# Retention core of a two-layer hybrid trunk: a chunk's rows are normalised on ScalarE, with scale and bias made on GpSimd

## The chip, the cores and the metric

One core of a Trainium2 chip runs the whole program. The metric is device time in microseconds (us); before the change it is 3035.81 us, the median of 3 runs (3035.24 to 3036.67). TensorE is called PE in the profile, its weight loads PEld, VectorE DVE, ScalarE ACT, GpSimd POOL, and SyncE SP; SP and ACT also issue DMAs.

## The reference, cut to what matters

The trunk has two layers. Layer 0 mixes with a gated delta net, layer 1 with retention, and each is followed by a residual layer norm and a convolutional FFN. Only the retention of layer 1 is touched (4 heads, key width 256, value width 512, 8 chunks of 128 rows):

```
def retention(h, w_in, w_out):
    ...
    scores = jnp.einsum('bhncd,bhnmd->bhncm', q, k) * dmask[None, :, None]
    intra = jnp.einsum('bhncm,bhnmv->bhncv', scores, v)
    def step(state, inp):
        q_n, k_n, v_n = inp
        o = jnp.einsum('bhck,bhkv->bhcv', q_n, state) * xi[None, :, :, None]
        state = (state * gamma_c[None, :, None, None]
                 + jnp.einsum('bhck,bhcv->bhkv', k_n * zeta[None, :, :, None], v_n))
        return state, o
    ...
    o = _unchunk_heads(intra + jnp.moveaxis(inter, 0, 2))
    o = _standardize(o, 1e-6).reshape(b_, s, H * dv)
    o = o * jax.nn.silu(gate.astype(F32))
    return o.astype(h.dtype) @ w_out
```

`_standardize(o, 1e-6)` subtracts each row's mean over its 512 values and multiplies by one over the root of variance plus 1e-6. The change is in how this is done on the chip.

## The kernel before

Activations and weights are split into a high and a low part, and a product is three matmuls (low by high, high by low, high by high). In the retention stage (about 1800 to 2190 us of the span) two kinds of work share the engines:

- `ret_fill` is the filler on TensorE: the value projection `ret_v` for each head and half (weights are loaded into `wr`, split into `wh` by ScalarE and `wl` by VectorE, and the products split again into `vv`), and after the last head the first part of the output projection (`ab`, `bb`).
- `core(h)` goes through the 8 chunks of head h in order. This text numbers the chunks 0 to 31, so that chunk 7 is the last of the first head. For chunk n it makes the state update in two tiles `p2` (matmuls `sc<-vv,kz`, three for each tile), calls `ret_front` for chunk n+1 (scores `sT`, their split `sThl`, the scaled keys `kz`, and on GpSimd the scaled queries `qx`), and then makes the chunk's output `po`.
- `ret_back(h, n, po)` takes `po` (128 rows of 512, in PSUM) through the normalisation into `on`, transposes `on` on TensorE (`mm<-cst,on`), multiplies by the gate rows `gt` into `ot` on VectorE, and stores `ot`. From chunk 4 of each head on, GpSimd also makes four sums and differences of `ot` and of an earlier block `op` that is loaded again (the loop with `pool.tensor_tensor(d, x, y, op)`, written `ot<-ot`, `op<-ot,op`, `op<-op` and `ot<-ot,op` in the profile); the output projection reads these from DRAM.

`po` and `p2` share two PSUM buffers (tag `sc`). In the order of use, the second `p2` tile of a chunk takes the buffer of the `po` just before it, so its first matmul must wait until the last reader of that `po`, which is the instruction that writes `on`.

TensorE's order in this stage is written down by the kernel: `run` picks the next piece of work by a model clock, and `pm` and `ptr` chain every matmul and transpose to the one before (`pq`). The delays after which a piece may go on are the numbers `RL`; the transposes of `on` are placed `RL["b"]` = 3.21 us of model time behind `po`. None of these numbers changes. All engines take their instructions in a fixed order; that of VectorE, ScalarE, GpSimd and SP is decided when the program is built, by a scheduler that models the engines' times. So an instruction that waits on GpSimd also holds those behind it.

GpSimd has other work in the stage: `bg_gain` multiplies and adds gain rows (L381 and L382, 128x512 each) for a later residual, `qx` (L1689), and the sums above (L1775; L1777 in the changed file).

Of the kernel before, what the change touches and what calls it, by code (L numbers as in the profile page):

```python
# [11 lines left out]
AF = mybir.ActivationFunctionType  # L12
ALU = mybir.AluOpType
# [20 lines left out]
def trunk_kernel(ctx: ExitStack, tc, A):  # L34
    nc = tc.nc
    pe, act, dve, pool, sp = nc.tensor, nc.scalar, nc.vector, nc.gpsimd, nc.sync
# [9 lines left out]
    def tl(tag, shape, dt=F32, name=None):  # L46
        return sb.tile(shape, dt, tag=tag, name=name or tag, bufs=BUFS[tag])
# [7 lines left out]
    def ct(name, shape, dt=F32):  # L55
        return cp.tile(shape, dt, tag=name, name=name)
# [4 lines left out]
    def mm_tile():  # L61
        return ps.tile([P, HALF], F32, tag="mm", name="mm", bufs=2)
# [13 lines left out]
    def v4(ap):  # L76
        return ap.rearrange("p (c f) -> p c f", f=P)
# [66 lines left out]
    mhalf = ct("mhalf", [P, NCH])  # L144
# [493 lines left out]
    def ptr(out, src):  # L638
        pq(pe.transpose(out, src, ident), 0.109)
# [4 lines left out]
    def emit(name, lat=0.0):  # L644
        events[name] = clk[0] + lat
# [1046 lines left out]
    def core(h):  # L1692
# [8 lines left out]
        for n in range(NCH):  # L1701
# [25 lines left out]
            if n > 0:  # L1727
                for j in range(2):
                    pm(po, r["qx"][:, j], St[:, j], start=False, stop=(j == 1), cost=0.857)
            give("qkv", 2)  # L1730
            yield [(-0.1, ret_back(h, n, po))]
            yield RL["c"]
            St, r = Sn, rn
        emit(("core", h))

    def ret_back(h, n, po):
        st = tl("st", [P, 2, 6], name="rst")
        dve.bn_stats(st[:, 0], po)
        mv = tl("s8", [P, 4], name="mv")
        dve.bn_aggr(mv[:, 0:2], st[:, 0])  # L1740
        dve.tensor_scalar(mv[:, 2:3], mv[:, 1:2], 1e-6, None, ALU.add)
        pool.tensor_tensor(mv[:, 3:4], mv[:, 2:3], mhalf[:, 0:1], ALU.pow)
        on = tl("t2", [P, HALF], name="on")
        dve.tensor_scalar(on, po, mv[:, 0:1], mv[:, 3:4], ALU.subtract, ALU.mult)
        yield RL["b"]
        sl = slice(n * P, (n + 1) * P)
        g = tl("cv", [P, 516], name="gt")[:, 0:HALF]
        sp.dma_start(v4(g), gd[4 * h:4 * h + 4, :, sl].rearrange("j p t -> p j t"))
        pt = mm_tile()
        for j in range(4):  # L1750
            ptr(pt[:, j * P:(j + 1) * P], on[:, j * P:(j + 1) * P])
        ot = tl("cv", [P, 516], name="ot")[:, 0:HALF]
        dve.tensor_mul(ot, pt, g)
        s4 = slice(n % 4 * P, (n % 4 + 1) * P)

        def pair_view(t):
            return t.rearrange("p (j a f) -> p a j f", a=2, f=P)

        def blk(nm):
            return od[2 * h:2 * h + 2, ABLK.index(nm), :, s4].rearrange("j p t -> p j t")  # L1760

        ov = pair_view(ot)
        if n < 4:
            for a, nm in enumerate(("11", "12")):
                anchor["x", 1] = act.dma_start(blk(nm), ov[:, a])
            if n == 3:
                emit(("ob", h), RL["o"])
            return
        pv = pair_view(tl("cv", [P, 516], name="op")[:, 0:HALF])
        for a, nm in enumerate(("11", "12")):  # L1770
            sp.dma_start(pv[:, a], blk(nm))
        act.dma_start(blk("22"), ov[:, 1])
        for d, x, y, op, nm in ((ov[:, 0], ov[:, 0], ov[:, 1], ALU.add, "S1"), (pv[:, 0], ov[:, 0], pv[:, 0], ALU.subtract, "S2"),
                                (pv[:, 1], pv[:, 1], pv[:, 0], ALU.subtract, "S4"), (ov[:, 1], ov[:, 1], pv[:, 0], ALU.subtract, "S3")):
            pool.tensor_tensor(d, x, y, op)  # L1775
            sp.dma_start(blk(nm), d)
# [135 lines left out]
```

## Time and profile before

| what | value |
|---|---|
| median of 3 runs | 3035.81 us |
| span of the profiled execution (first to last instruction) | 3033.2 us |
| PE busy, share of the span | 2841.1 us, 94% |
| DVE busy | 2303.6 us, 76% |
| ACT busy | 1314.4 us, 43% |
| POOL busy | 671.3 us, 22% |
| mean granted TensorE clock | 0.977 |

The profile lists one execution. Its span is 2.6 us below the median of the timed runs; the rest of a run's time lies outside the first and the last instruction. In rows of the timeline the columns are: start, duration (both us from the span's start), engine, line, operation, output and inputs, shapes and how many instructions in a row were merged; a bracket gives the idle time of the engine just before and what ended it. In rows of the groups they are: line, engine, operation, names, shapes and count, then the total busy time and the mean in ns, then idle time before and who ended it. Rows of the waits give the total, the number of times and the longest.

### The profile page before, as it was taken

Reading aid. Unit: us, or ns where it says so; the run is one execution under the profiler, and the core shown is the slowest. Engines: PE = TensorE matmul, PEld = TensorE weight load, DVE = VectorE, ACT = ScalarE, POOL = GpSimd, SP = SyncE. Lnnn points to the kernel's source line nnn. Section 1 sums busy time; section 2 is a strip of 40 time slices with the busy share of each in tenths; the row PEclk is TensorE's granted clock in tenths of the full one; section 3 lists DMA queues with packets and bytes.
Section 4 is the critical chain, followed back from the end, with each engine's and each line's share of the span. In section 5 each row is a group of like instructions: output and inputs, shape, how many; then the busy total and the mean of one; then the engine's idle time right before and its main releaser. Section 6 shows DMA issues by size and latency. Waiting matters only on the chain.

```text
span 3033.2 us, 39037 instructions
## 1 busy us (share of the span) xinstructions
PE 2841.1 (94%) x13590; PEld 2309.7 (76%) x13590; DVE 2303.6 (76%) x3971; ACT 1314.4 (43%) x2408; POOL 671.3 (22%) x637
## 2 busy tenths in 40 slices
PE   8999899999999999998999999999998899999996
PEld 7877777877778888776777787767776678887885
DVE  5878788565888888988688645666788887777988
ACT  4745555434544444535333342222344544444442
POOL 0312211043021111820023302432200011113604
PEclk9999999999999999999999999999999999999998
DMA  7231222254354445854322544656654243335663
GB/s 275 78 122 53 77 84 78 88 176 144 107 169 149 148 150 170 316 176 154 132 100 89 174 163 138 209 178 178 214 199 150 90 144 104 105 105 202 238 192 122
DMA packets 243028, 450.23 MB, mean 148 GB/s; under 512 B 22928, under 2 KB 76432, under 8 KB 242832
## 3 DMA queue, kind: packets, MB, share of 16 engines
q1 hardware_dynamic: 211648, 400.02, 40.2%
q10 hardware_dynamic: 29760, 43.00, 3.9%
q0 software_dynamic: 1424, 4.72, 0.4%
q8 instruction: 107, 1.75, 0.2%
q14 instruction: 89, 0.73, 0.1%
HBM read 339.13 MB, written 108.53 MB: 148 GB/s over the span
## 4 chain that ended last, share of the span: by engine, by line
PE 55%; DVE 22%; DMA 11%; issue 6%; ACT 4%; POOL 2%; SPq 0%; POOLq 0%; DVEq 0%; ACTq 0%
PE acc L636 11%; PE acc L1148 7%; PE acc L110 4%; PE acc L111 4%; PE acc L112 4%; PE sc L636 4%; PE sc L1148 3%; DMA mvw<-in_ada_w 2%; PE acc L278 2%; PE acc L279 2%; PE acc L280 2%; PE mm L636 2%; DMA wr<-in_ffn_up 2%; DVE qkv L457 2%; DVE wb L90 2%
## 5 line engine op out<-in xcount | busy, mean ns | idle before, releaser
L636 PE MATMUL acc<-hT,wh 128*128 128x512 f32 x960 | 299.4, 393 | 0.0
L1546 POOL TENSOR_TENSOR o<-o 128x512 f32<-128x512 f32 x88 | 118.0, 1352 | 721.5 <-DVE o L1539 680.5
L278 PE MATMUL acc<-bb,ab 128*128 128x512 f32 x504 | 190.5, 406 | 33.5 <-DVE ab L90 20.4
L1148 PE MATMUL acc<-T,wb 128*128 128x512 f32 x840 | 206.0, 393 | 10.3 <-DVE wb L90 10.0
L279 PE MATMUL acc<-bb,ab 128*128 128x512 f32 x504 | 204.5, 406 | 8.8 <-DVE bb L90 8.5
L636 PEld LDWEIGHTS acc<-hT,wh 128*128 128x128 f32 x960 | 181.8, 189 | 34.1
L89 ACT ACTIVATE ab<-ar 128x512 fp32r<-128x512 f32 x210 | 128.6, 624 | 168.0 <-PE acc L280 83.7
L636 PE MATMUL acc<-hT,wl 128*128 128x512 f32 x480 | 201.2, 419 | 0.1
L280 PE MATMUL acc<-bb,ab 128*128 128x512 f32 x504 | 200.9, 400 | 0.0
L1148 PEld LDWEIGHTS acc<-T,wb 128*128 128x128 f32 x840 | 157.9, 189 | 48.4 <-DVE wb L90 14.7
L90 DVE TENSOR_TENSOR ab<-ar,ab 128x512 fp32r<-128x512 f32 x210 | 167.9, 809 | 34.5 <-ACT ab L89 34.1
L90 DVE TENSOR_TENSOR wl<-wr,wh 128x1024 fp32r<-128x1024 f32 x85 | 108.7, 1279 | 97.2 <-ACT wh L89 96.4
L90 DVE TENSOR_TENSOR wb<-wr,wb 128x512 fp32r<-128x512 f32 x162 | 114.5, 709 | 87.7 <-ACT wb L89 85.2
L90 DVE TENSOR_TENSOR wb<-mm,wb 128x512 fp32r<-128x512 f32 x216 | 145.0, 683 | 17.5 <-ACT wb L89 15.6
L89 ACT ACTIVATE wh<-wr 128x1024 fp32r<-128x1024 f32 x101 | 106.8, 1059 | 111.2 <-PE acc L636 43.4
L89 ACT ACTIVATE wb<-mm 128x512 fp32r<-128x512 f32 x216 | 122.8, 594 | 66.6 <-DVE mm L1194 65.5
L1205 ACT ACTIVATE pc<-acc 128x512 f32<-128x512 f32 x143 | 84.4, 592 | 147.1 <-PE acc L1148 92.5
L278 PEld LDWEIGHTS acc<-bb,ab 128*128 128x128 f32 x504 | 96.9, 194 | 62.5 <-DVE ab L90 20.3
L1525 DVE SCALAR_TENSOR_TENSOR o<-g,vc,o 128x512 f32<-128x512 f32 (+2 forms) x176 | 136.6, 795 | 5.1 <-ACT o L1520 4.5
L636 PE MATMUL acc<-wh,hT 128*128 128x512 f32 x384 | 137.2, 420 | 2.0 <-DVE vv L90 2.0
L89 ACT ACTIVATE wb<-wr 128x512 fp32r<-128x512 f32 x162 | 98.8, 626 | 87.0 <-DMA wr<-in_ffn_up 47.2
L216 DVE SCALAR_TENSOR_TENSOR ada<-mvw,e,ada 128x512 f32<-128x512 f32 x140 | 107.7, 769 | 29.0 <-DMA mvw<-in_ada_w 28.7
(636 smaller groups left out, 7855.7 us busy)
## 6 DMA issues: line engine op xcount, KB each, us to landing
wr<-in_ffn_up SPq DMA_DIRECT2D x96, 512.0 KB, 4.2
mvw<-in_ada_w SPq DMA_DIRECT2D x80, 512.0 KB, 4.3
ad<-o SPq DMA_DIRECT2D x154, 256.0 KB, 2.6
ar<-ad SPq DMA_DIRECT2D x154, 256.0 KB, 4.3
Br<-in_ffn_down SPq DMA_DIRECT2D x88, 256.0 KB, 3.7
wr<-in_ret_wv SPq DMA_DIRECT2D x32, 512.0 KB, 3.6
ar<-od SPq DMA_DIRECT2D x56, 256.0 KB, 5.3
xs<-xt ACTq DMA_DIRECT2D x24, 512.0 KB, 3.9
```

Of the source, the lines that this page charges most:

```text
L89: act.activation(dst_h, src, AF.Copy)
L90: eng.tensor_tensor(dst_l, src, dst_h, ALU.subtract)
L110: mm(acc, wl[:, k], hl[0], start=first, stop=False)
L111: mm(acc, wh[:, k], hl[1], start=False, stop=False)
L112: mm(acc, wh[:, k], hl[0], start=False, stop=last)
L278: mm(acc, a[1][:, sl], w[0], start=first, stop=False)
L279: mm(acc, a[0][:, sl], w[1], start=False, stop=False)
L280: mm(acc, a[0][:, sl], w[0], start=False, stop=last)
L636: pq(pe.matmul(out, lhsT, rhs, start=start, stop=stop), cost)
L1148: return pe.matmul(*a, skip_group_check=True, **kw)
L1525: dve.scalar_tensor_tensor(tv, gv[:, c0 - j:c1 - j], w[:, 2 - j:3 - j], tv, ALU.mult, ALU.add)
L1546: pool.tensor_tensor(o[d], o[x], o[y], op)
```

## The change

VectorE keeps the statistics (`bn_stats`, `bn_aggr`, the added epsilon) and gets one more small instruction, the negated mean. GpSimd makes the inverse root as before and then multiplies it by the negated mean, which gives the bias. ScalarE writes `on` as Identity(scale * po + bias), where VectorE wrote it with a subtraction and a multiplication.

```
         dve.bn_aggr(mv[:, 0:2], st[:, 0])
-        dve.tensor_scalar(mv[:, 2:3], mv[:, 1:2], 1e-6, None, ALU.add)
-        pool.tensor_tensor(mv[:, 3:4], mv[:, 2:3], mhalf[:, 0:1], ALU.pow)
+        dve.tensor_scalar(mv[:, 1:2], mv[:, 1:2], 1e-6, None, ALU.add)
+        dve.tensor_scalar(mv[:, 2:3], mv[:, 0:1], -1.0, None, ALU.mult)
+        pool.tensor_tensor(mv[:, 3:4], mv[:, 1:2], mhalf[:, 0:1], ALU.pow)
+        pool.tensor_tensor(mv[:, 2:3], mv[:, 2:3], mv[:, 3:4], ALU.mult)
         on = tl("t2", [P, HALF], name="on")
-        dve.tensor_scalar(on, po, mv[:, 0:1], mv[:, 3:4], ALU.subtract, ALU.mult)
+        act.activation(on, po, AF.Identity, bias=mv[:, 2:3], scale=mv[:, 3:4])
```

The lines of the power are L1742 before and L1743 after; the new multiplication on GpSimd is L1744 after, and `on` is L1744 before and L1746 after. TensorE's order in the retention core is the same in both programs. The order of the other engines is not, and the places that matter follow.

GpSimd at chunk 0, before (`mv<-mv,mhalf` is the power, `xg` the gain rows, `qx` the scaled queries):

```order
L1689 TENSOR_TENSOR qx<-qk,dx 128x128 x2
L381 TENSOR_TENSOR xg<-xg,gb 128x512
L1742 TENSOR_TENSOR mv<-mv,mhalf 128x1
L382 TENSOR_TENSOR xg<-xg,gb 128x512
L1689 TENSOR_TENSOR qx<-qk,dx 128x128 x4
```

The same place after (`mv<-mv` is the new multiplication):

```order
L1689 TENSOR_TENSOR qx<-qk,dx 128x128 x2
L381 TENSOR_TENSOR xg<-xg,gb 128x512
L1743 TENSOR_TENSOR mv<-mv,mhalf 128x1
L382 TENSOR_TENSOR xg<-xg,gb 128x512
L1744 TENSOR_TENSOR mv<-mv 128x1
L1689 TENSOR_TENSOR qx<-qk,dx 128x128 x4
```

The multiplication stands behind the gain rows' addition, and not right behind the power. Chunk 8 has the same order.

GpSimd at chunk 7, the last of the first head, before:

```order
L1775 TENSOR_TENSOR ot<-ot 128x2x128
L1742 TENSOR_TENSOR mv<-mv,mhalf 128x1
L381 TENSOR_TENSOR xg<-xg,gb 128x512 x2
L1775 TENSOR_TENSOR op<-ot,op 128x2x128
L382 TENSOR_TENSOR xg<-xg,gb 128x512 x2
```

And after:

```order
L1777 TENSOR_TENSOR ot<-ot 128x2x128
L1743 TENSOR_TENSOR mv<-mv,mhalf 128x1
L381 TENSOR_TENSOR xg<-xg,gb 128x512 x2
L1777 TENSOR_TENSOR op<-ot,op 128x2x128
L1744 TENSOR_TENSOR mv<-mv 128x1
L382 TENSOR_TENSOR xg<-xg,gb 128x512 x2
```

Here the multiplication stands behind two gain rows' products and one difference. At chunks 15, 23, 29 and 31 one `op<-ot,op` stands between the power and the multiplication.

ScalarE at chunk 0, after (`wh`, `kz`, `sThl` and `vv` are the splits and scalings named above); before, the same rows stand there without `on` (L1746):

```order
L89 ACTIVATE wh<-wr 128x1024
L1746 ACTIVATE on<-sc,mv 128x512
L1680 ACTIVATE kz<-mm,vc 128x256
L1767 DMA od<-ot 128x2x128 x2
L89 ACTIVATE sThl<-sT 128x128
L89 ACTIVATE vv<-acc 128x512 x2
L1746 ACTIVATE on<-sc,mv 128x512
```

`on` of chunk 0 stands ahead of the scaled keys, and `on` of chunk 1 between the splits of the values.

## The prediction

> **What bounds the kernel now.** I read the page first, then the waits of the retention stage, then the timeline around single chunks.
>
> ```profile
> span 3033.2 us, 39037 instructions
> PE 2841.1 (94%) x13590; PEld 2309.7 (76%) x13590; DVE 2303.6 (76%) x3971; ACT 1314.4 (43%) x2408; POOL 671.3 (22%) x637
> ```
>
> TensorE is the bound of the whole. The stage that changes is 345 us of it (busy time by engine with counts, then clock and DMA):
>
> ```profile
> 1840.00:2185.00 345.00, 322.72 (x1422) 247.69 (x1421) 222.07 (x403) 80.53 (x140) 121.28 (x167) 0.98 0.61 187
> ```
>
> TensorE is busy for 322.7 us, VectorE for 222.1, ScalarE for 80.5. VectorE has 120 us to spare, so work taken from it gains only what TensorE waits for. TensorE's order here is fixed, so each of its waits lengthens the run, and what the change can win is in the waits for `on`:
>
> ```profile
> DVE on L1744 <- POOL mv L1742: 31.6, 26, 4.6
> PE sc L636 <- DVE on L1744: 7.8, 4, 4.4
> PE mm L639 <- DVE on L1744: 6.3, 3, 3.3
> ```
>
> TensorE waits for `on` in 7 of 32 chunks, 14.1 us in all: 4 times for the PSUM buffer that `on` sets free (chunks 3, 5, 13, 20; rows below), 3 times to transpose `on` (chunks 7, 15, 31). VectorE in turn stands idle 31.6 us until the power on GpSimd is done.
>
> **The change part by part.** What is removed from VectorE, what is added, and the nearest rows for the new ones:
>
> ```profile
> L1744 DVE TENSOR_SCALAR on<-sc,mv 128x512 f32<-128x512 f32 x32 | 25.9, 809 | 31.6 <-POOL mv L1742 31.6
> L1741 DVE TENSOR_SCALAR mv<-mv 128x1 f32<-128x1 f32 x32 | 4.9, 154 | 1.1
> L1689 POOL TENSOR_TENSOR qx<-qk,dx 128x128 f32<-128x128 f32 x56 | 27.1, 505 | 126.1 <-DMA qk<-qd 81.9 <-PE sc L636 44.1
> L1775 POOL TENSOR_TENSOR ot<-ot 128x256 f32<-128x256 f32 x16 | 12.1, 756 | 37.3 <-DVE ot L1753 34.6 <-DVE mv L1740 2.6
> L261 ACT ACTIVATE t<-mm,fh,fs 128x512 f32<-128x512 f32 x28 | 20.9, 773 | 17.6 <-PE mm L259 10.5 <-DVE hT L90 7.2
> ```
>
> - VectorE loses 32 times 0.81 us and the idle 31.6 us before it, and gets 32 times 0.15 us for the negated mean. That one runs while GpSimd makes the power, so it is off the chain. Net it is free for some 52 us, at no direct gain.
> - The new multiplication on GpSimd, 128x1, is not in the trace. From 128 to 256 elements a GpSimd instruction grows by 756 - 505 = 251 ns, so one element should take some 505 - 251 = 254 ns: my estimate is 0.25 us. The upper bound is the power itself, 0.55 us.
> - ScalarE's `on` has the form of L261 (Identity from PSUM, scale and bias by row): 0.77 us, where VectorE took 0.81. No table load is added.
>
> A chunk without trouble, chunk 1:
>
> ```profile
> 1851.90 0.70 DVE L1738 BATCH_NORM_STATS2 rst<-sc 128x6 f32<-128x512 f32 x1 [0.36 <-PE sc L636]
> 1853.09 0.55 POOL L1742 TENSOR_TENSOR mv<-mv,mhalf 128x1 f32<-128x1 f32 x1 [0.26 <-DVE mv L1741]
> 1853.67 0.81 DVE L1744 TENSOR_SCALAR on<-sc,mv 128x512 f32<-128x512 f32 x1 [0.67 <-POOL mv L1742]
> 1855.15 1.52 PE L636 MATMUL sc<-vv,kz 128*128 128x512 f32 x6
> 1857.17 0.60 PE L639 MATMUL mm<-cst,on 128*128 128x128 f32 x4
> ```
>
> From the power's end (1853.64) to the end of `on` (1854.48) it is 0.84 us. Afterwards it is 0.25 + 0.04 + 0.77 = 1.06, with a hand-over between the two GpSimd instructions some 0.3 more than now. The buffer is needed by the fourth of the six state matmuls (1855.15 + 3 x 0.23 = 1855.84, 1.4 us after `on`), and the transposes come 2.7 us after it. So in most chunks the longer chain costs nothing. It costs where TensorE already waits for the buffer (chunks 3, 5, 13 and 20: 4 x 0.3 = 1.2 us),
>
> ```profile
> 1878.34 1.22 PE L636 MATMUL sc<-vv,kz 128*128 128x512 f32 x2 [4.35 <-DVE on L1744]
> 1899.99 0.97 PE L636 MATMUL sc<-vv,kz 128*128 128x512 f32 x3 [0.81 <-DVE on L1744]
> 1985.79 0.96 PE L636 MATMUL sc<-vv,kz 128*128 128x512 f32 x3 [0.83 <-DVE on L1744]
> 2067.65 1.26 PE L636 MATMUL sc<-vv,kz 128*128 128x512 f32 x3 [1.80 <-DVE on L1744]
> ```
>
> and where the multiplication does not follow the power at once.
>
> Chunks 0 and 8: the addition of gain rows (L382) now stands between.
>
> ```profile
> 1845.76 1.28 POOL L382 TENSOR_TENSOR xg<-xg,gb 128x512 f32<-128x512 f32 x1
> 1846.12 1.54 PE L636 MATMUL sc<-vv,kz 128*128 128x512 f32 x6
> 1938.71 1.29 POOL L382 TENSOR_TENSOR xg<-xg,gb 128x512 f32<-128x512 f32 x1
> 1939.08 1.54 PE L636 MATMUL sc<-vv,kz 128*128 128x512 f32 x6
> ```
>
> L382 ends at 1847.04; plus 1.06 gives an `on` that ends at 1848.1. The fourth matmul ran at 1846.12 + 0.69 = 1846.81. That is 1.3 us of waiting where there was none; chunk 8 likewise (1940.00 + 1.06 = 1941.06 against 1939.77), 1.3 us.
>
> Chunk 7: two gain products and a difference stand between, and TensorE waits there already.
>
> ```profile
> 1916.35 0.55 POOL L1742 TENSOR_TENSOR mv<-mv,mhalf 128x1 f32<-128x1 f32 x1
> 1916.87 3.48 POOL L381 TENSOR_TENSOR xg<-xg,gb 128x512 f32<-128x512 f32 x2
> 1920.31 0.73 POOL L1775 TENSOR_TENSOR op<-ot,op 128x256 f32<-128x256 f32 x1
> 1916.94 0.81 DVE L1744 TENSOR_SCALAR on<-sc,mv 128x512 f32<-128x512 f32 x1 [2.12 <-POOL mv L1742]
> 1917.89 1.05 PE L639 MATMUL mm<-cst,on 128*128 128x128 f32 x4 [3.25 <-DVE on L1744]
> ```
>
> The difference ends at 1921.04, `on` at 1922.1, and the transposes start 0.15 later, as they do now behind 1916.94 + 0.81 = 1917.75: at 1922.25 and not 1917.89, 4.4 us. The two gain products took 3.48 us, though one alone takes 1.3; unslowed it would be 3.5 us. I take 4.0.
>
> Chunks 15, 29 and 31: one difference (`op<-ot,op`) stands between.
>
> ```profile
> 2002.18 0.73 POOL L1775 TENSOR_TENSOR op<-ot,op 128x256 f32<-128x256 f32 x1 [0.97 <-POOL mv L1742]
> 2002.53 0.63 PE L639 MATMUL mm<-cst,on 128*128 128x128 f32 x4 [0.74 <-DVE on L1744]
> 2162.17 0.96 POOL L1775 TENSOR_TENSOR op<-ot,op 128x256 f32<-128x256 f32 x1 [1.23 <-DMA op<-od]
> 2162.34 1.52 PE L636 MATMUL sc<-vv,kz 128*128 128x512 f32 x6
> 2180.28 0.73 POOL L1775 TENSOR_TENSOR op<-ot,op 128x256 f32<-128x256 f32 x1
> 2181.25 0.63 PE L639 MATMUL mm<-cst,on 128*128 128x128 f32 x4 [2.32 <-DVE on L1744]
> ```
>
> Chunk 15: 2002.91 + 1.06 + 0.15 = 2004.1 against 2002.53, 1.6 us. Chunk 29: the difference itself waits for a DMA; 2163.13 + 1.06 = 2164.2 against the fourth matmul at 2162.34 + 0.68 = 2163.02, 1.2 us. Chunk 31: 2181.01 + 1.06 + 0.15 = 2182.2 against 2181.25, 1.0 us. At chunk 23 the difference was done early enough that I put nothing.
>
> What is queued behind: GpSimd's gain rows, `qx` and differences move by 0.25 us each time, and `qx` is needed a chunk later. On ScalarE, `kz`, `wh` or `vv` stand behind an `on` that waits; `kz` waits for the transposed keys anyway. Sum of the stalls: 1.2 + 1.3 + 1.3 + 4.0 + 1.6 + 1.2 + 1.0 = 11.6 us.
>
> TensorE's clock comes on top. After stalls it runs at half for a while (stretches of the span; the last three figures of a row are the clock, the DMA share and GB/s):
>
> ```profile
> 1876.98:1883.81 6.83, 5.47 (x18) 4.81 (x19) 3.38 (x6) 0.47 (x1) 2.33 (x3) 0.50 0.63 191
> 1917.94:1921.35 3.41, 3.41 (x11) 2.84 (x12) 1.87 (x2) 0.00 (x0) 3.41 (x4) 0.50 0.56 141
> 2181.00:2185.00 4.00, 3.75 (x19) 3.19 (x20) 2.73 (x5) 0.95 (x2) 3.11 (x4) 1.00 0.70 208
> ```
>
> The 4.35 us stall of chunk 3 cost 5.47 / 2 = 2.7 us of half clock, the 3.25 us stall of chunk 7 cost 3.41 / 2 = 1.7, the 2.32 us stall of chunk 31 nothing. Chunk 7's stall grows to 7 us (2.7 where it was 1.7), chunk 31's to 3.3 (perhaps 1.7 where it was none). I add 2.0, between 0 and 4. The Trainium skill, TensorE: Matmul & The Clock Gate, Part 1, has the gate fall to half after an idle window of about 3.4 us and rise after a busy one of the same length. By that, chunk 7 would pay one such window however long it idles, chunk 31 none, the clock would add nothing, and the time would be 3035.8 + 11.6 = 3047.4. The stall of 3.25 us, below 3.4, and the 6.83 us at half clock speak for counting less strictly.
>
> In all 11.6 + 2.0 = 13.6 us. The profiled span is 2.6 us below the median of the runs (3035.8 us), and I leave that offset as it is: 3035.8 + 13.6 = 3049.4, so 3049 us. About 0.2%, 6 us, is what a measurement of this kernel can tell from no change.
>
> **The rivals.**
>
> - *ScalarE becomes the queue that holds TensorE.* An `on` that waits 1 to 4 us for GpSimd stands ahead of `vv`, `wh` or `kz` on ScalarE; a late `vv` keeps an accumulator from the next projection. With GpSimd's multiplication at 0.55 us (0.3 more in ten chunks, 3 us) and some 1.2 us in each of four heads (5 us), the time is 3049 + 8 = 3057. For it: ScalarE is strictly in order. Against: it is busy 80.5 of 345 us.
> - *The delays are swallowed.* If GpSimd's neighbours run earlier because the gain rows and reloads arrive by DMA and not by TensorE's progress, chunk 7, 15, 29 and 31 lose most of their terms; 1.2 + 1.3 + 1.3 and a little remain, say 4 us: 3040. Against: those loads are issued behind stores that wait for TensorE's chunks.
> - *VectorE's relief wins, and the run is faster.* Its 31.6 us of idling ahead of `on` blocked splits (`wl`, `vv`) and with them later statistics. If half of the 14.1 us that TensorE waits for `on` came from statistics that start late, 7 us go: 3029. It decides where `bn_stats` starts more than 0.3 us earlier than now in a chunk that stalls. Against: in chunk 7 the power itself was late on GpSimd, not VectorE.
>
> That the change does not do what it says can be left out: the instructions stand in the changed order as written.
>
> **How the numbers follow.** Forecast 0.58, ScalarE's queue 0.14, swallowed 0.16, faster 0.12. The range reaches from the swallowed case with a little less (3038) to ScalarE's queue with the full clock term (3057 + 2, and some for chunks where I put nothing: 3062); faster is left out. Faster by over 0.2%: 0.12. Within 0.2% (up to 3041.9): the swallowed case, 0.16. Slower: 0.72.
>
> **What would show it.** TensorE's waits for `on` (now ScalarE's line L1746) should rise from 14 us to about 26, with new ones near chunks 0, 8 and 29 and a wait of 7 us at chunk 7. ScalarE's `on` should take about 0.77 us and wait for L1744 on GpSimd; that line should take about 0.25 us, and 0.55 would make every term longer. VectorE should no longer idle for L1742. If the waits for `on` fall below 14 us, the prediction is wrong in its main step; if they rise and the time does not, they were swallowed later.

## The result

The change makes the kernel slower: 3061.68 us, median of 4 runs (3057.34 to 3064.49), against 3036.24 us for the kernel before beside it (4 runs), a ratio of 1.0074 with a 95% interval of 1.0061 to 1.0086. That is 25.4 us where 13.2 were forecast (from 3035.8 to 3049); the time lies 0.3 us below the upper end of the range. In a later comparison the same pair gave 3055.48 against 3036.84 us, 1.0071 (1.0051 to 1.0090).

The page of the changed kernel begins so; TensorE's busy time has grown by 12.7 us for the same 13590 matmuls:

```profile
span 3061.6 us, 39170 instructions
PE 2853.8 (93%) x13590; PEld 2321.1 (76%) x13590; DVE 2282.8 (75%) x3971; ACT 1335.0 (44%) x2440; POOL 682.1 (22%) x669
```

The waits of the retention stage after the change (total us, how often, the longest):

```profile
POOL mv L1743 <- DVE mv L1742: 85.2, 21, 13.0
ACT on L1746 <- POOL mv L1744: 61.9, 22, 6.6
PE mm L639 <- ACT on L1746: 14.0, 4, 7.5
PE sc L636 <- ACT on L1746: 13.6, 8, 4.6
```

TensorE now waits 27.6 us for `on`, where it waited 14.1 and about 26 were forecast. Its rows at chunks 0, 7, 8 and 15:

```profile
1853.87 1.25 PE L636 MATMUL sc<-vv,kz 128*128 128x512 f32 x3 [2.12 <-ACT on L1746]
...
1930.52 1.12 PE L639 MATMUL mm<-cst,on 128*128 128x128 f32 x4 [7.50 <-ACT on L1746]
...
1955.83 0.96 PE L636 MATMUL sc<-vv,kz 128*128 128x512 f32 x3 [2.15 <-ACT on L1746]
...
2023.13 1.11 PE L639 MATMUL mm<-cst,on 128*128 128x128 f32 x4 [2.65 <-ACT on L1746]
```

To see where the time went, cut the span at matmuls that are the same in both programs. The core below is 1500 matmuls of TensorE, in the same order before and after. Busy time by engine over it, with counts, then clock, DMA share and GB/s; before:

```profile
1831.82:2194.22 362.40, 340.12 (x1501) 262.18 (x1500) 230.81 (x414) 85.42 (x148) 123.89 (x170) 0.98 0.60 184
```

After:

```profile
1836.60:2219.13 382.53, 350.74 (x1501) 268.74 (x1500) 210.55 (x414) 107.34 (x180) 130.13 (x202) 0.94 0.58 179
```

The core takes 20.1 us more: 10.6 more of busy time (340.12 to 350.74), which for the same matmuls is the lower clock, and 9.5 more of stalls (22.28 to 31.79, elapsed less busy). Ahead of the core, where the instructions are the same, the changed kernel is 4.8 us late already (1836.60 against 1831.82). That start lies between 1824.9 and 1837.3 us over all profiles of this study, with no tie to the change. Another 4.8 us are lost in a later stage (told below); the remainder of the span gains 1.3.

GpSimd's multiplication (L1744) and ScalarE's `on` (L1746), grouped by line and shape:

```profile
L1746 ACT ACTIVATE on<-sc,mv 128x512 f32<-128x512 f32 x32 | 24.8, 774 | 61.9 <-POOL mv L1744 61.9
L1744 POOL TENSOR_TENSOR mv<-mv 128x1 f32<-128x1 f32 x32 | 11.8, 370 | 1.9
```

`on` costs the 0.77 us that were expected. The multiplication has a mean of 0.37, and a mean can hide two kinds. Its shortest, median and longest duration in ns:

```profile
L1744 POOL TENSOR_TENSOR mv<-mv x32: 188/195/1255, 1851.8 to 2201.8; 128x1 f32<-128x1 f32 x32
```

In 25 chunks it takes 0.19 to 0.20 us; in five (0, 8, 11, 15 and 19) it takes 1.17 to 1.26, at chunk 31 it takes 0.64 and at chunk 27 0.30. In all seven a split of VectorE runs beside it. GpSimd and VectorE at chunk 0 show how:

```profile
1850.05 0.56 POOL L1743 TENSOR_TENSOR mv<-mv,mhalf 128x1 f32<-128x1 f32 x1 [0.51 <-DVE mv L1742]
1850.59 1.28 POOL L382 TENSOR_TENSOR xg<-xg,gb 128x512 f32<-128x512 f32 x1
1851.83 1.17 POOL L1744 TENSOR_TENSOR mv<-mv 128x1 f32<-128x1 f32 x1
...
1850.89 2.06 DVE L90 TENSOR_TENSOR wl<-wr,wh 128x1024 fp32r<-128x1024 f32 x1 [0.86 <-ACT wh L89]
```

Before, `on` stood ahead of the split `wl` on VectorE and waited there for the power:

```profile
1845.82 0.81 DVE L1744 TENSOR_SCALAR on<-sc,mv 128x512 f32<-128x512 f32 x1 [0.68 <-POOL mv L1742]
...
1846.55 1.58 DVE L90 TENSOR_TENSOR wl<-wr,wh 128x1024 fp32r<-128x1024 f32 x1
```

After, `wl` starts at 1850.89, while GpSimd adds gain rows. `wl` takes 1.21 us where it came first (chunk 20 below); here it takes 2.06 and ends at 1852.95, and the multiplication of one element per row, begun at 1851.83, ends at 1853.00 with it. The two engines held each other up in turn. At chunk 20 the same meets the power:

```profile
2083.18 1.52 POOL L1743 TENSOR_TENSOR mv<-mv,mhalf 128x1 f32<-128x1 f32 x1 [10.13 <-DVE mv L1742]
...
2083.07 1.21 DVE L90 TENSOR_TENSOR wl<-wr,wh 128x1024 fp32r<-128x1024 f32 x1
```

The power took 1.52 us and not 0.55, until `wl` was done. Before the change no `wl` ran beside a power. The power took 0.54 to 0.56 us in all 32 chunks of the first profile and in 31 of the second, where it took 0.93 at chunk 29, beside the split `bb`. Beside `vv` and `Sr`, which read one of their two tensors from PSUM, the multiplication kept its 0.195 us (chunks 6, 13 and 20). At chunks 11 and 19 its 1.25 us cost TensorE no wait. The Trainium skill, GPSIMD Engine Reference, Key points, names such a contention, for VectorE instructions with two SBUF inputs or in a two-port mode, and SBUF — State Buffer, Terms, says that the loser stands still for the whole instruction. `wl` has two such inputs, and the rows of both chunks agree.

### The profile page after: what moved, and what is told of

Its sections match the earlier page's. It is cut to its first block, busy times and chain, and to the rows that moved or that the text cites. A ratio compares the mean times of both kernels' runs of the same rounds, so it can differ in the third digit from the quotient of the medians.

```text
span 3061.6 us, 39170 instructions
## 1 busy us (share of the span) xinstructions
PE 2853.8 (93%) x13590; PEld 2321.1 (76%) x13590; DVE 2282.8 (75%) x3971; ACT 1335.0 (44%) x2440; POOL 682.1 (22%) x669
## 3 DMA queue, kind: packets, MB, share of 16 engines
q8 instruction: 107, 1.75, 0.2%
## 4 chain that ended last, share of the span: by engine, by line
PE 58%; DVE 21%; DMA 9%; issue 6%; ACT 4%; POOL 2%; SPq 0%; POOLq 0%; DVEq 0%; ACTq 0%
PE acc L636 14%; PE acc L1148 7%; PE acc L110 4%; PE acc L111 4%; PE acc L112 4%; PE sc L1148 4%; PE sc L636 3%; PE acc L278 2%; PE mm L636 2%; PE acc L280 2%; PE acc L279 2%; DVE bb L90 2%; DVE ab L90 2%; PE sc L110 1%; PE sc L111 1%
## 5 line engine op out<-in xcount | busy, mean ns | idle before, releaser
L279 PE MATMUL acc<-bb,ab 128*128 128x512 f32 x504 | 204.6, 406 | 10.3 <-DVE bb L90 10.2
L90 DVE TENSOR_TENSOR wb<-mm,wb 128x512 fp32r<-128x512 f32 x216 | 144.9, 683 | 17.4 <-ACT wb L89 15.6
```

The lines of the kernel that those rows point to most:

```text
L90: eng.tensor_tensor(dst_l, src, dst_h, ALU.subtract)
L279: mm(acc, a[0][:, sl], w[1], start=False, stop=False)
```

## The experiments

The theories, named as in the expectations: **A**, the multiplication is reached late because gain rows or a difference stand ahead of it on GpSimd, in six chunks; **B**, ScalarE's queue holds `on`, or what stands behind it; **C**, the time is lost elsewhere; and, after the first four runs, **D**, A together with the hold-up between GpSimd and VectorE. All times follow, each beside runs of the kernel before on the same chip; core and busy are those of the profiled run, over the 1500 matmuls. The two profiles of before give 362.4 and 365.8 us, mean 364.1, those of the change 382.5 and 383.1, mean 382.8. So two profiles of one kernel can differ by 3.4 us.

| kernel | median us | before | ratio (95%) | core | PE busy in it |
|---|---|---|---|---|---|
| bias_on_vector | 3054.16 | 3038.31 | 1.0049 (1.0034 to 1.0065) | 371.07 | 342.52 |
| bias_on_gpsimd_rows_on_vector | 3057.19 | 3038.31 | 1.0062 (1.0045 to 1.0079) | 383.40 | 347.20 |
| change_in_six_chunks | 3050.91 | 3038.31 | 1.0043 (1.0029 to 1.0056) | 373.39 | 342.84 |
| change_in_other_chunks | 3046.17 | 3038.31 | 1.0016 (1.0003 to 1.0029) | 370.36 | 343.10 |
| bias_on_scalar | 3048.68 | 3039.10 | 1.0038 (1.0020 to 1.0057) | 371.10 | 342.81 |
| bias_one_input | 3044.90 | 3039.10 | 1.0032 (1.0016 to 1.0048) | 365.51 | 342.10 |
| before_gain_late | 3038.15 | 3039.10 | 1.0001 (0.9988 to 1.0014) | 363.05 | 340.30 |
| before_again | 3043.53 | 3039.10 | one run | 365.79 | 342.20 |
| after_again | 3055.48 | 3036.84 | 1.0071 (1.0051 to 1.0090) | 383.09 | 349.18 |
| after_late_transposes | 3055.03 | 3036.84 | 1.0060 (1.0040 to 1.0080) | 380.25 | 345.88 |
| before_late_transposes | 3039.51 | 3036.84 | 1.0007 (0.9995 to 1.0019) | 361.29 | 341.14 |
| bias_one_input_late_transposes | 3052.80 | 3036.84 | 1.0052 (1.0034 to 1.0069) | 377.69 | 345.77 |

**Rows on ScalarE, bias on VectorE** (bias_on_vector):

```
-        pool.tensor_tensor(mv[:, 2:3], mv[:, 2:3], mv[:, 3:4], ALU.mult)
+        dve.scalar_tensor_tensor(mv[:, 2:3], mv[:, 0:1], -1.0, mv[:, 3:4], ALU.mult, ALU.mult)
```

The negated mean is left out too, as this instruction holds the -1.

> The rows of a chunk are still normalised by ScalarE, but the bias is made by one VectorE instruction behind the power, so GpSimd has one instruction in a chunk, as before the change. Theory A (the loss comes from the multiplication, which GpSimd reaches only after gain rows or a difference at chunks 0, 7, 8, 15, 29, 31): the new stalls go, 0.2 to 0.3 us is added where TensorE already waits, 3036 to 3042 us; waits of TensorE for the normalised rows 14 to 17 us. Theory B (ScalarE's queue holds the rows back, and kz, wh and vv behind them): 3050 to 3062 us. Theory C (the time is lost elsewhere, in the clock or in stages that the change does not touch, whenever the program is shuffled): 3045 to 3060 us with waits for the rows that stay at 14 to 17 us.

Theory A's 3036 to 3042 fell: 3054 us, and TensorE waits 21.9 us for `on`. The time alone lies in the ranges of B and of C, but C's 14 to 17 us of waits fell too. The core lost 7.0 us over the mean of before, not 18.7. What is left is seen in the durations of the bias instruction (shortest, median, longest) and at chunk 0:

```profile
L1743 DVE SCALAR_TENSOR_TENSOR mv<-mv x32: 150/160/1239, 1851.3 to 2192.7; 128x1 f32<-128x1 f32 x32
```

```profile
1851.29 1.27 POOL L382 TENSOR_TENSOR xg<-xg,gb 128x512 f32<-128x512 f32 x1
...
1851.35 1.24 DVE L1743 SCALAR_TENSOR_TENSOR mv<-mv 128x1 f32<-128x1 f32 x1 [0.67 <-POOL mv L1742]
```

Now it is VectorE's 128x1 instruction that lasts until GpSimd's gain rows are done. It took 0.57 to 1.24 us in six chunks, 0, 7 and 8 among them, and 0.40 to 0.41 in five more, each time beside an instruction of GpSimd.

**Bias on GpSimd, rows on VectorE** (bias_on_gpsimd_rows_on_vector):

```
-        act.activation(on, po, AF.Identity, bias=mv[:, 2:3], scale=mv[:, 3:4])
+        dve.tensor_scalar(on, po, mv[:, 3:4], mv[:, 2:3], ALU.mult, ALU.add)
```

> GpSimd makes power and bias as in the change, but VectorE normalises the rows (scale and bias), as before the change. Theory A: the same stalls as in the change at the six chunks, 3050 to 3064 us, with a wait of about 7 us at chunk 7. Theory B: ScalarE's queue is relieved, 3037 to 3043 us. Theory C: 3045 to 3060 us without the stalls of the six chunks.

As A had it: 3057 us, a wait of 6.26 us at chunk 7, and a core as long as with the change, with nothing of it on ScalarE:

```profile
1829.31:2212.71 383.40, 347.20 (x1501) 266.17 (x1500) 231.14 (x446) 85.54 (x148) 129.85 (x202) 0.96 0.57 174
```

So GpSimd's second instruction is enough for a loss of this size, without the move of the rows to ScalarE. The parts are not all the same: chunk 23, for one, waits 2.17 us here and 0.56 with the change. The hold-up is here too, in the same five chunks, though VectorE still writes the rows, because `wl` now stands ahead of `on` in its order. Chunk 0:

```profile
1843.60 2.02 DVE L90 TENSOR_TENSOR wl<-wr,wh 128x1024 fp32r<-128x1024 f32 x1 [0.90 <-ACT wh L89]
...
1844.50 1.17 POOL L1744 TENSOR_TENSOR mv<-mv 128x1 f32<-128x1 f32 x1
...
1845.71 0.81 DVE L1746 TENSOR_SCALAR on<-sc,mv 128x512 f32<-128x512 f32 x1
```

It is VectorE's order, then, and not its relief from the rows, that brings `wl` beside the multiplication. Why the scheduler chose that order is not shown.

**The change in six chunks, and in the other 26** (change_in_six_chunks; change_in_other_chunks has `not in`):

```
+        if 8 * h + n in (0, 7, 8, 15, 29, 31):
             (the changed lines)
+        else:
             (the lines of before)
```

> The change is made in chunks 0, 7, 8, 15, 29 and 31 alone, the other 26 are as before it. Theory A: these six hold nearly all of the loss, some 12 us of stalls and 5 us of half clock, 3048 to 3058 us. Theory B: 6 chunks of 32 bear about a fifth of the loss, 3037 to 3042 us. Theory C: between, 3040 to 3055 us, with no tie to the stalls.

> The change is made in the 26 chunks other than 0, 7, 8, 15, 29 and 31. Theory A: only the longer chain at chunks 3, 5, 13 and 20 is left, about 1 us, 3034 to 3041 us. Theory B: four fifths of the loss, 3053 to 3060 us. Theory C: 3040 to 3055 us.

The six chunks cost 9.3 us of the core and 3050.9 us. The time is in A's range, but 7.6 us of the 9.3 are stalls and 1.7 the clock, where A gave some 12 and 5. The other 26 cost 6.3 us of the core where A gave 1, and 3046.2 us where A gave at most 3041; that time is a weak witness, as the interval of its ratio reaches from 1 to 9 us over before. Among them are chunk 20, whose power was held by `wl` again (1.52 us; TensorE waits 2.86 us), and chunk 6, where TensorE had not waited before:

```profile
1909.51 0.66 PE L639 MATMUL mm<-cst,on 128*128 128x128 f32 x4 [1.46 <-ACT on L1747]
```

Chunk 6 is not on A's list, but there too a sum stands between power and multiplication, and it waits for a store:

```profile
1907.77 0.72 POOL L1782 TENSOR_TENSOR ot<-ot,op 128x256 f32<-128x256 f32 x1 [2.08 <-DMA od<-ot]
1908.45 0.20 POOL L1746 TENSOR_TENSOR mv<-mv 128x1 f32<-128x1 f32 x1
```

As they were worded, neither A nor B holds alone; the two parts make 15.6 of the 18.7 us.

**Bias on ScalarE, GpSimd with the power alone** (bias_on_scalar):

```
-        pool.tensor_tensor(mv[:, 2:3], mv[:, 2:3], mv[:, 3:4], ALU.mult)
+        act.activation(mv[:, 2:3], mv[:, 2:3], AF.Copy, scale=mv[:, 3:4])
```

> As the change, but the bias is made by a ScalarE instruction of 128x1 right ahead of the one that normalises; GpSimd makes the power alone, VectorE does nothing behind the power. Theory D (the cost is GpSimd's second instruction, by its place behind gain rows and differences and by GpSimd and VectorE holding each other up: where a split of VectorE runs, GpSimd's 128x1 multiplication took 1.2 us and not 0.2): TensorE's retention core, 362.4 us before and 382.5 after, comes to 364 to 368 us, the run 2 to 6 us over the kernel before. Theory B (ScalarE's queue): the core comes to 372 us or more, the run at least 10 us over the kernel before.

371.1 us lies between D (364 to 368) and B (372 or more), and so does the run, 9.6 us over before by the medians (D 2 to 6, B 10 or more). Most of the loss went with GpSimd's instruction, but ScalarE's queue has a price. At chunk 0:

```profile
1845.94 0.29 ACT L1744 ACTIVATE mv<-mv 128x1 f32<-128x1 f32 x1 [2.69 <-POOL mv L1743]
1846.15 1.04 ACT L89 ACTIVATE wh<-wr 128x1024 fp32r<-128x1024 f32 x1
1847.09 0.76 ACT L1746 ACTIVATE on<-sc,mv 128x512 f32<-128x512 f32 x1
```

The bias waits in place for the power, and the split `wh`, which used that time before, now stands between bias and `on`; TensorE waits 0.76 us there and 0.85 at chunk 8.

**Bias on VectorE by an instruction with one tensor input** (bias_one_input):

```
-        dve.scalar_tensor_tensor(mv[:, 2:3], mv[:, 0:1], -1.0, mv[:, 3:4], ALU.mult, ALU.mult)
+        dve.tensor_scalar(mv[:, 2:3], mv[:, 0:1], mv[:, 3:4], -1.0, ALU.mult, ALU.mult)
```

> As the run with the bias on VectorE, but by an instruction that reads one tensor and takes the scale as a number for each row, where that run's reads two tensors. Theory D with the lock between GpSimd and VectorE (the Trainium skill, GPSIMD Engine Reference, puts it on VectorE instructions with two SBUF inputs or in a two-port mode): every bias instruction takes about 0.15 us, none 0.6 to 1.2 us as six did; the core falls from 371 to 366 to 369 us. If the lock does not matter: the core stays at 371 us, within 1 us.

```profile
L1743 DVE TENSOR_SCALAR mv<-mv x32: 203/214/215, 1848.6 to 2186.0; 128x1 f32<-128x1 f32 x32
```

```profile
1848.52 1.28 POOL L382 TENSOR_TENSOR xg<-xg,gb 128x512 f32<-128x512 f32 x1
...
1848.58 0.21 DVE L1743 TENSOR_SCALAR mv<-mv 128x1 f32<-128x1 f32 x1 [0.67 <-POOL mv L1742]
...
1847.77 1.06 ACT L89 ACTIVATE wh<-wr 128x1024 fp32r<-128x1024 f32 x1 [1.94 <-PE acc L636]
1848.82 0.78 ACT L1745 ACTIVATE on<-sc,mv 128x512 f32<-128x512 f32 x1
```

At the same place, beside the same gain rows, the bias takes 0.21 us, though not the 0.15 expected, and in all 32 chunks none took longer than 0.215. `wh` runs while the power is made, and `on` follows at once. The core falls from 371.1 to 365.5 us, half a us below what D gave and inside what the kernel before shows. This is the run that shows the hold-up as a cause: same engine, same work, one tensor input less, 5.6 us. In the core TensorE and VectorE have the same order in both runs; GpSimd and ScalarE each have one instruction moved, at chunk 6. TensorE's waits at chunks 0, 8 and 7, where the bias was held longest, fall by 1.03, 0.91 and 1.35 us, 3.3 together; the rest is less than what two profiles of one kernel can differ by. It also shows that the rows on ScalarE cost the core next to nothing when scale and bias come in time. The whole is still 0.32% slower than before.

**Gain rows one step later, in the kernel before** (before_gain_late: each step loads a gain row and then works on the row of the step before):

```
             sp.dma_start(x, src[rs, hs(c)])
-            pool.tensor_tensor(x, x, gb[0], ALU.mult)
-            ...
+            flush()
+            late.append((x, gb[0], gb[1], dst[rs, hs(c)]))
```

> The kernel before, with the gain rows of the next stage multiplied one step later than they are loaded, so that GpSimd need not wait for the load. Theory D (GpSimd's order decides when a chunk is normalised): the 4.35 us wait of chunk 3, where the gain row's load held GpSimd ahead of the power, falls below 1.5 us with its 2.7 us of half clock, chunk 7's 3.25 us may fall too; 5 to 9 us faster than before. Rival: the work that is put off meets the power in another chunk, and the time stays within 3 us.

The rival holds: 1.0001. Chunk 3 still waits 4.34 us, because GpSimd still waits for a load there:

```profile
1864.92 2.25 POOL L377 TENSOR_TENSOR xg<-xg,gb 128x512 f32<-128x512 f32 x1 [9.10 <-DMA xg<-xs]
...
1870.00 0.55 POOL L1753 TENSOR_TENSOR mv<-mv,mhalf 128x1 f32<-128x1 f32 x1
```

The chain that ends there leads back to the store of an earlier gain row, 7.58 us long, which frees the load's buffer. Working later does not make the buffer free sooner.

**The kernel before and the change once more**:

> The kernel before once more, for a second profile of it: is the stall of 3.5 us at about 2440 us, in every profile but that of before, a consequence of the change or a matter of the single run? If of the run: it shows here too, or the stage from matmul 10800 to 11400 takes 150 to 153 us and not 149.1. The core takes 362 to 364 us in both cases.

> The change once more, for a second profile and for times beside the other variants. If what was told of it holds, its retention core takes 380 to 385 us (382.5 in the first profile; the kernel before took 362.4 and 365.8 in its two), GpSimd's bias instruction takes over 1.1 us at chunks 0, 8 and 15 again, and the time is 18 to 28 us over the kernel before. If the first profile was an odd one, the core comes below 376 us.

The change's core repeats, 383.1 us. That of before comes to 365.8, above the 362 to 364 expected. The bias took 1.17 to 1.25 us at chunks 0, 8, 11, 15 and 19 again. The stall of 3.5 us near 2440 us is not one of the run: before has none above 2.3 us there in either profile, the change has it in both.

**Transposes of `on` 2 us later** (`RL["b"]` 5.2 and not 3.21), in the change, in the kernel before, and with the one-input bias:

> The change with the transposes of each chunk's rows placed some 2 us later in TensorE's order (RL b 5.2 instead of 3.21). If the last chunk of a head is lost to the late rows alone, its waits fall by 2 us each (7.5 at chunk 7, 2.65 at chunk 15, 3.3 at chunk 31, 0.6 at chunk 23 vanishes): 6 us of stalls and 2 to 4 of half clock less, 12 to 18 us over the kernel before. Rival: chunk 7 is held by GpSimd's queue, which waits for what TensorE does next, and the shuffled order gives back what it wins: within 4 us of the change.

> The kernel before with the transposes placed 2 us later (RL b 5.2). Its waits at chunks 7, 15 and 31 (3.25, 0.74 and 2.32 us) fall to about 1.3, 0 and 0.3: 4 to 5 us of stalls and up to 2 of half clock less, 3031 to 3035 us if the kernel before stands at 3038. Rival: nothing is won, within 3 us of before.

> Rows on ScalarE, bias by the VectorE instruction with one input, transposes placed 2 us later. The waits at the last chunks (4.7, 0.9, 1.0 and 2.3 us) fall by up to 2 us each, 5 us in all: as fast as the kernel before, from 4 us below to 4 us above it. Rival: 6 to 10 us over it, as without the later transposes.

Nothing was won. With the change the time is 18.2 us over before, just above the 12 to 18 expected, and within 4 us of the change, the rival's case: chunk 7 still waits 7.72 us, and though chunk 15 falls to 0.69 and the waits of chunks 23 and 31 vanish, one of 3.72 us for `vv` comes up. Before's waits at chunks 7, 15 and 31 shrink (chunk 7 to 1.87), but new ones of 3.25 and 2.55 us for `vv` come up. With the one-input bias both expectations missed, 16 us over before: its core has new or longer waits for `vv` (3.92 and 2.52 us) and, at two chunks, for `on` (2.97 and 2.61). Why these two combine so badly was not followed up. No version beats the kernel before.

## The loss behind the core

From the 11101st to the 11251st matmul, some 230 us behind the core, the changed kernel takes 4.8 us more, before first and then after:

```profile
2426.24:2461.31 35.07, 34.90 (x151) 28.23 (x150) 30.91 (x46) 17.25 (x29) 7.53 (x6) 1.00 0.55 186
```

```profile
2450.35:2490.19 39.84, 36.35 (x152) 29.23 (x150) 33.81 (x52) 19.34 (x34) 7.37 (x6) 0.96 0.55 181
```

ScalarE there, before:

```profile
2424.35 1.09 ACT L89 ACTIVATE wb<-mm 128x512 fp32r<-128x512 f32 x2 [5.12 <-DVE mm L1194]
2425.32 0.72 ACT L1520 ACTIVATE o<-g,vc 128x512 f32<-128x512 f32 x1
```

After, with TensorE's row:

```profile
2449.93 0.72 ACT L1520 ACTIVATE o<-g,vc 128x512 f32<-128x512 f32 x1 [5.06 <-DMA ad<-o]
2450.56 1.06 ACT L89 ACTIVATE wb<-mm 128x512 fp32r<-128x512 f32 x2
...
2454.45 4.08 PE L1148 MATMUL sc<-T,wb 128*128 128x512 f32 x10 [3.49 <-DVE wb L90]
```

The lines are not edited, but their order is another: after, `o`, which waits 5.06 us for a store, stands ahead of two splits that TensorE needs. The order of ScalarE's instructions is made when the program is built and came out differently far behind the edit. Both profiles of before take 35 us for this stretch, before_gain_late 36.3, all others, with the change or another one, 38.2 to 41.0 us (before_late_transposes 39.85). In those eleven `o` stands ahead of the two splits, in the other three behind them. So these 3 to 5 us go with that order, and not with what the change does in the core: before_late_transposes pays them with the rows and the statistics as before. No run puts the order back by itself. They are also over half of what bias_one_input loses.

## Why the prediction was right or wrong

*Direction and main mechanism: right.* The multiplication queues behind GpSimd's other work where the orders said so. At chunk 7, two gain rows and a difference stand between power and bias:

```profile
1925.83 0.55 POOL L1743 TENSOR_TENSOR mv<-mv,mhalf 128x1 f32<-128x1 f32 x1
1926.34 2.48 POOL L381 TENSOR_TENSOR xg<-xg,gb 128x512 f32<-128x512 f32 x2
1928.78 0.72 POOL L1777 TENSOR_TENSOR op<-ot,op 128x256 f32<-128x256 f32 x1
1929.46 0.19 POOL L1744 TENSOR_TENSOR mv<-mv 128x1 f32<-128x1 f32 x1
```

*The stalls, 11.6 us: right in sum, less so in their parts.* Growth of each wait in the first pair of profiles, and in the second:

| chunk | forecast | first | second |
|---|---|---|---|
| 0 | 1.3 | 2.12 | 2.15 |
| 8 | 1.3 | 2.15 | 2.14 |
| 7 | 4.0 | 4.25 | 3.46 |
| 15 | 1.6 | 1.91 | 1.98 |
| 29 | 1.2 | 0.37 | 1.02 |
| 31 | 1.0 | 0.97 | 0.64 |
| 3, 5, 13, 20 | 1.2 | 0.98 | 2.37 |

They make 12.8 and 13.8 us. Chunks 0 and 8 cost over 0.8 more each, about the 0.92 us by which the multiplication, held by `wl`, outlasts my estimate of 0.25: the bound of 0.55 for it was wrong. Smaller growth elsewhere (chunks 29 and 31, in the second pair chunk 7) makes up a part, so that the sum is still near is partly luck. Not in the sum were chunk 23 (0.56, 1.04), chunk 6 (0.97 in the second profile), and a gain: the wait of 3.02 us for `Sr` at 2022 us of the kernel before is gone in both profiles of the change. Net, the core's stalls grow by 9.5 and 10.3 us.

*The clock, 2.0 us: the term that was mis-sized.* TensorE's busy time in the core grew by 10.6 us (340.12 to 350.74), in the second pair by 7.0 (342.20 to 349.18). I let only stalls count that were long already. But stalls of 2 us do it as well; these stretches at half clock go with the waits of chunks 0, 7 and 8:

```profile
1854.38:1857.79 3.41, 3.41 (x14) 3.12 (x14) 1.19 (x2) 0.47 (x1) 0.00 (x0) 0.50 0.65 211
1926.06:1936.30 10.24, 5.78 (x16) 4.73 (x17) 0.69 (x1) 0.78 (x1) 8.89 (x12) 0.50 0.64 198
1956.78:1960.19 3.41, 3.41 (x15) 3.12 (x14) 1.96 (x4) 0.47 (x1) 0.00 (x0) 0.50 0.51 180
```

Waits of 2.12 and 2.15 us cost 3.41 us at half clock each, half of which is lost, nearly as much again as the wait. The profile of the kernel before had shown it already, behind the wait of 1.80 us at chunk 20, and I overlooked it:

```profile
2068.13:2071.54 3.41, 3.41 (x15) 3.11 (x14) 2.25 (x4) 0.47 (x1) 0.00 (x0) 0.50 0.64 234
```

Size alone does not decide. Over the cores of all 14 profiles, a stretch at half clock began within 39 of the 57 waits of 1.80 to 3.12 us or at most 3.5 us behind them; in the first profile of the kernel before, waits of 2.32 and 2.74 us had none. All 33 longer waits had one, and none of the 21 from 1.2 to 1.75 us. In each profile all changes of the clock lie on one grid of 3.41 us, so where a wait falls on it may decide; that was not tested. By the rule that the prediction cited from the Trainium skill (TensorE: Matmul & The Clock Gate, Part 1) the clock would have added nothing; the traces do not agree with that use of it.

*The order behind the core, 4.8 us: not in the sum at all.* I compared the orders at the places of the edit only.

*The range: held by luck.* Its upper end, 3062, was worked out from ScalarE's queue as the rival. The runs do not bear that rival out for the change, and the time came in 0.3 us below 3062 for other reasons: the clock, the hold-up and the order behind the core.

*The rivals.* ScalarE's queue shows no net cost in the change itself (the core is as long with the rows on VectorE) and some in bias_on_scalar. VectorE's relief turned round: `wl`, run where VectorE had waited for the power, came beside GpSimd's small instructions and is a part of the loss.

*What stays open.* The 20.1 us of the first pair and the 4.8 behind the core make 24.9 where the medians differ by 25.4, but so close a fit is chance. The two profiled spans differ by 28.4 us, which includes 4.8 ahead of the core and 1.3 gained behind it. In the second pair the medians differ by 18.6 us and the spans by 10.5: 17.3 in the core and 4.9 behind it, less 7.4 ahead of the core and 4.3 elsewhere. Stretches with unchanged instructions differ by several us from profile to profile, so single us are not assigned. The split of the loss between place and hold-up on GpSimd was not measured by itself. An estimate from the durations of the first profile: the multiplication outlasts its 0.195 us by 0.98 at chunks 0, 8 and 15 and by 0.44 at chunk 31, and the power its 0.55 by 0.97 at chunk 20, which is 4.3 of the 12.8 us of grown waits. The larger part would then be the place.

## What to carry to other kernels

Look at what an engine does with time that it is given back: an engine that waits in place may be keeping another's way free. An instruction of one element per row costs what it must wait for, and here that was six times itself; where VectorE and GpSimd share a stage, give VectorE's small ones on a chain a form with one tensor input. Count the clock as a likely cost on stalls from about 1.8 us on, as the waits of these profiles do, and compare the order of the whole program, not only of the edited lines.

## What the runs showed that I had not expected

- GpSimd's 128x1 multiplication takes 0.195 us alone and up to 1.26 us beside a VectorE instruction with two tensor inputs in SBUF, but 0.195 beside one that reads one of its two from PSUM; VectorE's 128x1 instruction with two inputs goes from 0.16 to 1.24 us beside GpSimd, with one input it stays at 0.20 to 0.215.
- Waits of TensorE of 1.8 to 3.1 us, and not only longer ones, had a stretch at half clock in or behind them, in 39 of 57 cases.
- An edit in one stage changed the order of ScalarE 230 us later and cost 3 to 5 us there.
